# Two layers of a hybrid diffusion backbone: banks, table loads and eviction order in the LRU stage

## The chip, the cores and the metric

One core of a Trainium2 chip runs the whole program in one launch. The metric is the device time of one execution in microseconds (us); several executions are timed and the median is taken. TensorE (PE) multiplies matrices into PSUM banks, VectorE (DVE) and ScalarE (ACT) read them and do the elementwise work, GpSimd (POOL) does little here, and SyncE (SP) issues the transfers. PEld is TensorE's loading of weights.

## What is computed

For 256 latent tokens and 256 context tokens of width 1024, each of two layers does this (the reference, cut; the attention branches and the feed-forward part are left as calls):

```python
h = _rmsnorm(x, lp['norm1_g']) * (1.0 + sc1) + sh1            # hc for the context tokens in the same way
rx, rg, cq, ckv, kr, dq, dk, dv, mg = _split_cols(h @ lp['w_in'], IN_SPLITS)
# RG-LRU branch
xr = _centred_dwconv(rx, lp['conv_w'], lp['conv_b'])
r = jax.nn.sigmoid(gr);  i = jax.nn.sigmoid(gi)               # gr, gi: block-diagonal products of xr
log_a = -LRU_C * r * jax.nn.softplus(-lam)
a = jnp.exp(log_a)
b = jnp.sqrt(-jnp.expm1(2.0 * log_a)) * i * xr
y_a = scan_forward(a[0], b[0]) + scan_backward(a[1], b[1])
# merge of the three branches
br_a = (y_a * jax.nn.gelu(rg)) @ lp['w_br_a']
br_b = o_b @ lp['w_br_b']                                      # latent attention
br_c = oc @ lp['w_br_c']                                       # differential attention
ga, gb, gc = jnp.split(jax.nn.sigmoid(mg), N_BRANCH, axis=-1)
x = x + g1 * ((ga * br_a + gb * br_b + gc * br_c) @ lp['w_out'])
x = x + g2 * _ffn(...)
```

The last layer needs the context tokens only as keys, values and start of the recurrence, so most of its products have 256 columns where the first layer's have 512.

## The kernel before

All products are made in split precision: `wload` fetches a weight block of 128x1024 float32, ACT copies it to a rounded half (`wh`) and DVE subtracts to get the rest (`wl`, both at L131 in `split`), and `mm3` (L192 to L194) issues three matmuls for each tile. A ring of three blocks (`WB`) holds weights; in the last layer two more lie in `room`, with two more staging blocks in the space of `acc`. A new block's transfer waits in SP's queue until DVE has split the block that used the same staging tile. Weight copies and splits are put 90 places ahead of program order (`WEIGHTS_FIRST`). The order of each engine's queue is made at build time by a scheduler that takes the ready instruction with the lowest order number; `tc.cur_priority` shifts that number. Once made, each engine runs its queue in order.

`gemm_fm` computes 256 output channels (two tiles j) over two weight blocks. In layer 0 (512 columns) the two tiles take a PSUM bank each, in layer 1 (256 columns) both share one, except rx's, which always has 512 columns. PSUM has eight banks: three with tag "mm" (`ps_mm`), two with tag "tr" (`ps_tr`, used by transposes), and three of a stage's own (`three_banks`).

The stage that the change is about comes after the differential attention's stage (the "pair" stage) and is called "single" (L1141). It loops over four pairs p of tiles. `rnn_rx` computes the recurrence's input for pair p+1 and `rnn_conv` evicts and convolves it (L1017 copies the bank to `xr` in layer 0, L1022 reads it). `rnn_rg` first runs `rnn_rec`: the two gates' products into the stage's own banks `pg`, Tanh (L1041), Exp (L1045), Tanh (L1046), then for the four results of the pair a Sqrt each (L1058), then multiplications (L1062) and scans (L1068) on DVE. Then it computes rg's product, and `gelu2` evicts it: Square (L1006, ACT), a product with the bank (L1007, DVE), Tanh (L1008, ACT), a product with the bank again (L1009, DVE). Between these, a queue of generators is worked off (`fill`): `branch_proj`, the differential branch's projection, read from its bank by DVE at L1107 together with its gate, and `branch_gate`, whose bank ACT reads with a Tanh into `gt` at L1099. The first gate and the first rx are already queued in the pair stage. All of these blocks use `ps_mm`. In layer 0 a slow background task (`mod_vectors`, L302) shares DVE.

ACT's functions come in table sets. The square root is in another set than Tanh and Exp, and a load is put by the compiler before the first function that needs another set. Copies, squares and the like need no particular set.

Of the kernel before, what the change touches and what calls it, by code (L numbers as in the profile page):

```python
# [13 lines left out]
AF = mybir.ActivationFunctionType  # L14
# [9 lines left out]
T = SEQ + CTX  # L24
# [32 lines left out]
WEIGHTS_FIRST = 90  # L57
NORMS_FIRST = 300
PAIR_FIRST = 2000


@with_exitstack
def tile_hybrid(ctx: ExitStack, tc: tile.TileContext, xt, cvec, cwide, prm, row, dlam, rope, wmod, wmod0, wmodt, wfm, wcq, wckv, wuq, wukv, wlru, wfo, out):
# [46 lines left out]
        return banks[0].tile([P, 512], F32, tag="sc", name=name, bufs=singles[0])  # L110

    turn = [0]

    def ps_any(name):

# [104 lines left out]
    def issue_after(b, a):  # L220

        tc.add_manual_dep(b.ins, a.ins.name, mybir.DependencyInfo(mybir.DependencyClass.NoSync, mybir.DependencyReason.DATA), reason="one table for all")
# [161 lines left out]
    def gemm_fm(l, widx, npair, xH, xL, TQ, ps_, consume, k_first=False):  # L384

        one = 2 * TQ <= 512
        for p in range(npair):
            if one:
                ps = ps_("ps0").rearrange("p (j n) -> p j n", j=2)
                pss = [ps[:, j, :] for j in range(2)]  # L390
            else:
                pss = [ps_(f"ps{j}")[:, :TQ] for j in range(2)]
            for hf in range(2):
                H, L = wload(*fm_block(l, widx, 2 * p + hf))
                H = H.rearrange("p (k n) -> p k n", n=256)
                L = L.rearrange("p (k n) -> p k n", n=256)
                order = [(j, kk) for kk in range(4) for j in range(2)] if k_first and p == 0 else [(j, kk) for j in range(2) for kk in range(4)]
                for i, (j, kk) in enumerate(order):
                    k = hf * 4 + kk
                    mm3(pss[j], H[:, kk, j * P:(j + 1) * P], L[:, kk, j * P:(j + 1) * P], xH[:, k, :TQ], xL[:, k, :TQ],  # L400
                        k == 0 and not (one and j == 1), k == KT - 1 and not (one and j == 0), one)
                    if k == KT - 1:
                        if not one:
                            consume(2 * p + j, 1, pss[j].unsqueeze(1))
                        elif j == 1:
                            consume(2 * p, 2, ps)
                    if i % 4 == 3 or k_first and p == 0 and i % 2 == 1:
                        yield (6 if k_first and p == 0 else 12) * mm_ns(TQ)
# [126 lines left out]
    for l in range(LAYERS):  # L535
# [7 lines left out]
        with ExitStack() as c1:  # L543
# [13 lines left out]
            def t_cq(name, dt=F32R):  # L557
                return tmp("cq", 10, dt=dt, name=name)
# [4 lines left out]
            def t_p(name):  # L563
                return tmp("p", 4, name=name)
# [448 lines left out]
            def rnn_conv(t, ps, st):  # L1013
                xr = ps
                if not last:
                    xr = t_p("xr")
                    A.activation(xr, ps, AF.Copy)  # L1017
                xc = t_cq("xc", F32)
                xr3 = xr.rearrange("p (s t) -> p s t", s=2)
                xc3 = xc.rearrange("p (s t) -> p s t", s=2)  # L1020
                w = [pm[:, CW + 8 * j + t:CW + 8 * j + t + 1] for j in range(4)]
                A.activation(xc, xr, AF.Identity, scale=w[2], bias=pm[:, CB + t:CB + t + 1])  # L1022
                for j in (0, 1, 3):
                    o_ = j - 2
                    d0, d1 = max(0, -o_), SEQ - max(0, o_)
                    V.scalar_tensor_tensor(out=xc3[:, :, d0:d1], in0=xr3[:, :, d0 + o_:d1 + o_], scalar=w[j], in1=xc3[:, :, d0:d1], op0=ALU.mult, op1=ALU.add)
                xH, xL = t_qk("xH"), t_qk("xL")
                split(xH, xL, xc)
                st.append((t, xc, xH, xL))

            def rnn_rec(pair, H, L):

                four = []
                for t, xc, xH, xL in pair:
                    for r in range(2):
                        th = []
                        for z in range(2):
                            pg = ps_sc("pg")
                            mm3(pg, H[:, z, r, t % 2, :], L[:, z, r, t % 2, :], xH, xL, True, True)
                            tz = t_pt("tz", F32)  # L1040
                            A.activation(tz, pg, AF.Tanh, scale=0.5, bias=hb[:, z, r, t:t + 1])  # L1041
                            th.append(tz)
                        a, tn = t_cq("a", F32), th[0]
                        sp = nsp[:, r, t:t + 1]
                        A.activation(a, th[0], AF.Exp, scale=sp, bias=sp)  # L1045
                        A.activation(tn, th[0], AF.Tanh, scale=sp, bias=sp)  # L1046
                        a2 = t_sc()
                        if last:
                            V.tensor_tensor(out=a2, in0=a, in1=a, op=ALU.mult)
                        else:  # L1050
                            A.activation(a2, a, AF.Square)
                        root = V.scalar_tensor_tensor(out=tn, in0=a2, scalar=1.0, in1=tn, op0=ALU.add, op1=ALU.mult)
                        g = xc if r else t_cq("g", F32)
                        V.scalar_tensor_tensor(out=g, in0=th[1], scalar=1.0, in1=xc, op0=ALU.add, op1=ALU.mult)
                        four.append((t, r, a, tn, g))
                        yield 6 * mm_ns(T)
                for t, r, a, tn, g in four:
                    issue_after(A.activation(tn, tn, AF.Sqrt, scale=-0.25), root)  # L1058
                lat, cx = slice(0, SEQ), slice(SEQ, T)
                hs = {}  # L1060
                for t, r, a, tn, g in four:
                    V.tensor_tensor(out=tn, in0=tn, in1=g, op=ALU.mult)  # L1062
                    hh = t_v("hh", F32)
                    for sl, h0 in ((cx, 0.0), (lat, hh[:, T - 1:T] if r == 0 else hh[:, SEQ:SEQ + 1])):
                        o_, a_, b_ = hh[:, sl], a[:, sl], tn[:, sl]
                        if r == 1:
                            o_, a_, b_ = o_[:, ::-1], a_[:, ::-1], b_[:, ::-1]
                        V.tensor_tensor_scan(out=o_, data0=a_, data1=b_, initial=h0, op0=ALU.mult, op1=ALU.add)  # L1068
                    if r == 0:
                        hs = hh  # L1070
                    else:
                        V.tensor_tensor(out=hs[:, :TQ], in0=hs[:, :TQ], in1=hh[:, :TQ], op=ALU.add)
                        st_y[t] = hs

            st_y = {}

            def rnn_rx(p, st):
                yield from gemm_fm(l, W_RX + p, 1, hH, hL, T, ps_mm, lambda j, n, ps: rnn_conv(2 * p + j, ps[:, 0, :], st))

            def rnn_rg(p):  # L1080
                H, L = wload(wlru[l, p])
                H = H.rearrange("p (z r n d) -> p z r n d", z=2, r=2, n=2)
                L = L.rearrange("p (z r n d) -> p z r n d", z=2, r=2, n=2)
                ge = {}
                yield from rnn_rec(rst[p], H, L)
                yield from gemm_fm(l, W_RG + p, 1, hH, hL, TQ, ps_mm, lambda j, n, ps: gelu2(j, n, ps, ge))
                for j in range(2):
                    t = 2 * p + j
                    V.tensor_tensor(out=ge[j], in0=ge[j], in1=st_y[t][:, :TQ], op=ALU.mult)
                    nc.sync.dma_start(yspill[:, t, :TQ], ge[j])  # L1090
# [4 lines left out]
            def branch_gate(mgi, p):  # L1095
                def gate(j, n, ps):
                    gt = t_v("gt", F32)[:, :n * TQ].rearrange("p (n c) -> p n c", n=n)
                    gts[mgi, 2 * p + j] = gt
                    A.activation(gt, ps, AF.Tanh, scale=0.5)  # L1099

                yield from gemm_fm(l, W_MG + mgi * 4 + p, 1, hH, hL, TQ, ps_mm, gate)

            def branch_proj(widx, mgi, p, after=None):
                def proj(j, n, ps):
                    t = 2 * p + j
                    gt = gts.pop((mgi, t))
                    V.scalar_tensor_tensor(out=gt, in0=gt, scalar=1.0, in1=ps, op0=ALU.add, op1=ALU.mult)  # L1107
                    V.tensor_tensor(out=acc[:, t:t + n, :TQ], in0=acc[:, t:t + n, :TQ], in1=gt, op=ALU.add)
                    if after is not None:
                        after(t + n - 1)  # L1110

                yield from gemm_fm(l, widx + p, 1, oH, oL, TQ, ps_mm, proj)

            three_banks(f"pair{l}")
            singles[0] = 1
# [24 lines left out]
            flush()  # L1140
            three_banks(f"single{l}")  # L1141
            singles[0] = 3

            c2.close()
            if not last:
# [322 lines left out]
```

## Time and profile before

| | |
|---|---|
| median of 3 runs | 1986.53 us (1986.1 to 1989.13) |
| the profiled execution | 1987.02 us |
| its span, first to last instruction | 1985.2 us |
| PE busy | 1935.7 us, 98% |
| DVE busy | 1570.4 us, 79% |
| ACT busy | 1070.8 us, 54% |
| POOL busy | 58.9 us, 3% |

All times in rows are from the start of the span. Matmuls are pipelined and their modelled ends overlap, so a PE that is busy all the time need not be at its peak. In a timeline, a row is a run of like instructions of one engine, and the bracket gives the idle time of the engine before it and whose signal ended that. A wait for several signals is put down to the one that came last. Layer 0's pair stage ends at about 555 us and its single stage runs from there; layer 1's single stage begins at about 1600 us.

### The profile page before, as it was taken

Reading aid. Unit: us, or ns where it says so; the run is one execution under the profiler, and the core shown is the slowest. Engines: PE = TensorE matmul, PEld = TensorE weight load, DVE = VectorE, ACT = ScalarE, POOL = GpSimd, SP = SyncE. Lnnn points to the kernel's source line nnn. Section 1 sums busy time; section 2 is a strip of 40 time slices with the busy share of each in tenths; the row PEclk is TensorE's granted clock in tenths of the full one; section 3 lists DMA queues with packets and bytes.
Section 4 is the critical chain, followed back from the end, with each engine's and each line's share of the span. In section 5 each row is a group of like instructions: output and inputs, shape, how many; then the busy total and the mean of one; then the engine's idle time right before and its main releaser. Section 6 shows DMA issues by size and latency. Waiting matters only on the chain. (4 is left out here: it accounts for less than half of the span.)

```text
span 1985.2 us, 31873 instructions
## 1 busy us (share of the span) xinstructions
PE 1935.7 (98%) x11746; PEld 1667.6 (84%) x11746; DVE 1570.4 (79%) x3870; ACT 1070.8 (54%) x1975; POOL 58.9 (3%) x198
## 2 busy tenths in 40 slices
PE   7999999999999999999999999999999999899999
PEld 4888888988677778888888888988999788898888
DVE  5679965888797787879888766898688889966763
ACT  4578833555576672343223224798444578855552
POOL 0001000000000000000000000012010000000000
PEclk9999999999999999999999999999999999999999
DMA  7211122112133356536665653412422134464553
GB/s 293 95 41 50 54 64 86 65 55 86 49 114 126 116 182 196 195 109 204 195 200 192 202 180 115 155 59 84 127 89 83 61 116 144 153 229 159 181 191 107
DMA packets 92028, 258.16 MB, mean 130 GB/s; under 512 B 10336, under 2 KB 17504, under 8 KB 91872
## 3 DMA queue, kind: packets, MB, share of 16 engines
q1 hardware_dynamic: 91872, 256.13, 39.2%
q8 instruction: 92, 1.51, 0.3%
q14 instruction: 64, 0.52, 0.1%
HBM read 250.85 MB, written 5.24 MB: 129 GB/s over the span
## 5 line engine op out<-in xcount | busy, mean ns | idle before, releaser
L131 ACT ACTIVATE wh<-st 128x1024 fp32r<-128x1024 f32 (+4 forms) x305 | 308.4, 1013 | 387.4 <-PE ps L193 188.6
L131 DVE TENSOR_TENSOR wl<-st,wh 128x1024 fp32r<-128x1024 f32 (+4 forms) x305 | 353.9, 1162 | 138.1 <-ACT wh L131 135.0
L192 PE MATMUL ps<-hH,wh 128*128 128x512 f32 (+1 forms) x512 | 187.3, 366 | 11.5 <-ACT gt L1099 8.8
L194 PE MATMUL ps<-hH,wl 128*128 128x512 f32 (+1 forms) x512 | 185.5, 363 | 4.5 <-DVE wl L131 4.5
L193 PE MATMUL ps<-hL,wh 128*128 128x512 f32 (+1 forms) x512 | 186.0, 363 | 0.0
L192 PE MATMUL pst<-wh,hH 128*128 128x256 f32 x568 | 164.4, 289 | 0.0
L193 PE MATMUL pst<-wl,hH 128*128 128x256 f32 x568 | 162.1, 285 | 0.0
L194 PE MATMUL pst<-wh,hL 128*128 128x256 f32 x568 | 162.0, 285 | 0.0
L192 PE MATMUL ps<-h2H,wh 128*128 128x512 f32 (+1 forms) x368 | 139.1, 381 | 0.6 <-ACT h2H L371 0.6
L193 PE MATMUL ps<-h2L,wh 128*128 128x512 f32 (+1 forms) x368 | 139.5, 380 | 0.0
L194 PE MATMUL ps<-h2H,wl 128*128 128x512 f32 (+1 forms) x368 | 139.5, 380 | 0.0
L613 DVE TENSOR_REDUCE st<-S 128x1 f32<-128x512 f32 (+1 forms) x192 | 112.9, 596 | 23.2 <-ACT dp L615 11.6
L192 PEld LDWEIGHTS ps<-hH,wh 128*128 128x128 f32 x512 | 98.4, 192 | 29.4 <-ACT gt L1099 10.9
L194 PEld LDWEIGHTS ps<-hH,wl 128*128 128x128 f32 x512 | 98.4, 192 | 19.7 <-DVE wl L131 5.9
L192 PEld LDWEIGHTS pst<-wh,hH 128*128 128x128 f32 x568 | 108.6, 191 | 3.8 <-issue 3.3
L131 DVE TENSOR_TENSOR room<-acc,room 128x1024 fp32r<-128x1024 f32 (+3 forms) x75 | 87.4, 1168 | 29.6 <-ACT room L131 28.3
L194 PEld LDWEIGHTS pst<-wh,hL 128*128 128x128 f32 x568 | 108.5, 191 | 1.7 <-issue 1.4
L193 PEld LDWEIGHTS ps<-hL,wh 128*128 128x128 f32 x512 | 98.6, 193 | 13.1
L193 PEld LDWEIGHTS pst<-wl,hH 128*128 128x128 f32 x568 | 108.6, 191 | 1.1 <-issue 0.7
L302 DVE SCALAR_TENSOR_TENSOR ms<-ms,cb 128x512 f32<-128x512 f32 x160 | 107.1, 686 | 1.3
L131 ACT ACTIVATE room<-acc 128x1024 fp32r<-128x1024 f32 (+3 forms) x75 | 76.2, 1017 | 57.0 <-PE ps L193 20.9
L302 DVE SCALAR_TENSOR_TENSOR sq<-ms,cb 128x512 f32<-128x512 f32 x112 | 75.5, 688 | 31.1 <-DMA ms<-wmodt 30.4
(586 smaller groups left out, 5542.6 us busy)
## 6 DMA issues: line engine op xcount, KB each, us to landing
st<-wfm SPq DMA_DIRECT2D x224, 512.0 KB, 3.5
ms<-wmodt SPq DMA_DIRECT2D x160, 256.0 KB, 2.8
acc<-wfm SPq DMA_DIRECT2D x56, 512.0 KB, 3.5
st<-wfo SPq DMA_DIRECT2D x35, 512.0 KB, 3.5
mstage<-wmod SPq DMA_DIRECT2D x16, 512.0 KB, 5.4
acc<-wfo SPq DMA_DIRECT2D x9, 512.0 KB, 3.5
st<-wlru SPq DMA_DIRECT2D x7, 512.0 KB, 3.4
st<-wukv SPq DMA_DIRECT2D x13, 256.0 KB, 2.5
```

The lines of the kernel that those rows point to most:

```text
L131: return A.activation(dH, src, AF.Copy), V.tensor_tensor(out=dL, in0=src, in1=f(dH), op=ALU.subtract)
L192: nc.tensor.matmul(ps, wH, xH, start=start, stop=False, skip_group_check=skip)
L193: nc.tensor.matmul(ps, wH, xL, start=False, stop=False, skip_group_check=skip)
L194: nc.tensor.matmul(ps, wL, xH, start=False, stop=stop, skip_group_check=skip)
L302: issue_after(V.scalar_tensor_tensor(out=o, in0=st, scalar=1.0, in1=cb[:, v, :], op0=ALU.mult, op1=ALU.mult, accum_out=sums[:, i - i0, h, ...
L613: V.tensor_reduce(out=st[:, 0:1], in_=S, axis=AX.X, op=ALU.max, negate=True)
```

## The change

Three things are changed, all for the blocks of the single stage.

The load of the table set with Tanh and Exp is written out, ordered behind the last of a group's four square roots, in `rnn_rec`.

rx, rg, gate and projection blocks take their banks in turn from five (`ps_five`: mm, tr, mm, tr, mm) from the start of the single stage on. Blocks started before, in the pair stage, keep `ps_mm`.

The order numbers of three kinds of evictions are lowered by 400 (`EVICT_FIRST`): the copy of rx's bank in layer 0, the gates' Tanh and the projections' read at L1107. The sum into `acc` behind that stays where it was.

```diff
+EVICT_FIRST = 400
...
+    five = [0]
+
+    def ps_five(name):
+
+        five[0] += 1
+        return (ps_mm, ps_tr, ps_mm, ps_tr, ps_mm)[(five[0] - 1) % 5](name)
...
                 if not last:
                     xr = t_p("xr")
+                    tc.cur_priority -= EVICT_FIRST
                     A.activation(xr, ps, AF.Copy)
+                    tc.cur_priority += EVICT_FIRST
...
                 for t, r, a, tn, g in four:
-                    issue_after(A.activation(tn, tn, AF.Sqrt, scale=-0.25), root)
+                    sq_ = A.activation(tn, tn, AF.Sqrt, scale=-0.25)
+                    issue_after(sq_, root)
+                issue_after(nc.scalar.preload_act_table_set("exp_and_others"), sq_)
...
+            ps_r = [ps_mm]
 
             def rnn_rx(p, st):
-                yield from gemm_fm(l, W_RX + p, 1, hH, hL, T, ps_mm, lambda j, n, ps: rnn_conv(2 * p + j, ps[:, 0, :], st))
+                yield from gemm_fm(l, W_RX + p, 1, hH, hL, T, ps_r[0], lambda j, n, ps: rnn_conv(2 * p + j, ps[:, 0, :], st))
...
-                yield from gemm_fm(l, W_RG + p, 1, hH, hL, TQ, ps_mm, lambda j, n, ps: gelu2(j, n, ps, ge))
+                yield from gemm_fm(l, W_RG + p, 1, hH, hL, TQ, ps_r[0], lambda j, n, ps: gelu2(j, n, ps, ge))
...
+                    tc.cur_priority -= EVICT_FIRST
                     A.activation(gt, ps, AF.Tanh, scale=0.5)
-
-                yield from gemm_fm(l, W_MG + mgi * 4 + p, 1, hH, hL, TQ, ps_mm, gate)
+                    tc.cur_priority += EVICT_FIRST
+
+                yield from gemm_fm(l, W_MG + mgi * 4 + p, 1, hH, hL, TQ, ps_r[0], gate)
...
+                    tc.cur_priority -= EVICT_FIRST
                     V.scalar_tensor_tensor(out=gt, in0=gt, scalar=1.0, in1=ps, op0=ALU.add, op1=ALU.mult)
+                    tc.cur_priority += EVICT_FIRST
...
-                yield from gemm_fm(l, widx + p, 1, oH, oL, TQ, ps_mm, proj)
+                yield from gemm_fm(l, widx + p, 1, oH, oL, TQ, ps_r[0], proj)
...
             three_banks(f"single{l}")
             singles[0] = 3
+            ps_r[0] = ps_five
```

## Rows read from the trace of the kernel before

**Rows 1.** The page's first part: busy us, share of the span, instructions.

```profile
PE 1935.7 (98%) x11746; PEld 1667.6 (84%) x11746; DVE 1570.4 (79%) x3870; ACT 1070.8 (54%) x1975; POOL 58.9 (3%) x198
```

**Rows 2.** Busy time by stretch: stretch, us, then each engine (instructions), clock, DMA.

```profile
core 0: us, PE busy (x) PEld busy (x) DVE busy (x) ACT busy (x) POOL busy (x), PEclk, DMA share, GB/s
555.00:790.00 235.00, 225.07 (x967) 181.76 (x966) 198.41 (x361) 142.62 (x208) 0.00 (x0) 0.99 0.45 148
1600.00:1725.00 125.00, 115.20 (x764) 104.46 (x764) 119.21 (x175) 105.50 (x146) 0.00 (x0) 1.00 0.40 131
```

**Rows 3.** PE's waits, 500 to 800 us: total us, times, longest.

```profile
PE ps L192 <- ACT gt L1099: 8.8, 5, 2.8
PE ps L192 <- DVE gt L1107: 2.7, 1, 2.7
```

**Rows 4.** Timeline of PE at the four longest of these: start, us, what.

```profile
529.57 0.50 PE L192 MATMUL ps<-hH,wh 128*128 128x512 f32 x1 [2.17 <-ACT gt L1099]
...
586.00 0.50 PE L192 MATMUL ps<-hH,wh 128*128 128x512 f32 x1 [2.83 <-ACT gt L1099]
...
638.78 0.50 PE L192 MATMUL ps<-hH,wh 128*128 128x512 f32 x1 [2.83 <-ACT gt L1099]
...
728.02 0.66 PE L192 MATMUL ps<-hH,wh 128*128 128x512 f32 x1 [2.67 <-DVE gt L1107]
```

**Rows 5.** PE's waits in layer 1's stage, 1590 to 1740 us.

```profile
PE ps L194 <- DVE room L131: 4.7, 3, 1.7
PE ps L194 <- DVE wl L131: 4.5, 2, 3.0
```

**Rows 6.** Busy time by stretch, 3.3 us behind PE's long waits (clock after POOL).

```profile
530.20:533.50 3.30, 3.30 (x13) 2.26 (x11) 1.26 (x4) 2.17 (x4) 0.00 (x0) 0.50 0.59 197
586.00:589.30 3.30, 3.30 (x14) 2.73 (x15) 2.80 (x4) 0.90 (x2) 0.00 (x0) 1.00 0.48 129
639.40:642.70 3.30, 3.30 (x9) 2.55 (x8) 3.30 (x8) 0.34 (x1) 0.00 (x0) 0.50 0.46 164
728.20:731.50 3.30, 3.30 (x9) 2.53 (x9) 3.30 (x6) 0.63 (x1) 0.00 (x0) 0.50 0.36 137
...
1724.90:1728.20 3.30, 3.30 (x18) 3.30 (x17) 3.30 (x7) 2.19 (x4) 0.00 (x0) 0.50 0.56 166
```

**Rows 7.** Timeline of DVE around 586 us: weight splits, ge's last reader.

```profile
586.40 1.20 DVE L131 TENSOR_TENSOR wl<-st,wh 128x1024 fp32r<-128x1024 f32 x1
...
589.50 0.69 DVE L1009 SCALAR_TENSOR_TENSOR ge<-ge,ps 128x512 f32<-128x512 f32 x1 [0.70 <-ACT ge L1008]
...
590.83 1.22 DVE L131 TENSOR_TENSOR wl<-st,wh 128x1024 fp32r<-128x1024 f32 x1
```

**Rows 8.** Timeline of ACT around 528 us and around 583 us.

```profile
527.21 1.06 ACT L131 ACTIVATE wh<-st 128x1024 fp32r<-128x1024 f32 x1 [2.19 <-PE ps L193]
528.18 0.76 ACT L615 ACTIVATE dp<-S,st,drq 128x512 f32<-128x512 f32 x1
...
528.93 0.58 ACT L1099 ACTIVATE gt<-ps 128x512 f32<-128x512 f32 x1
...
576.80 1.66 ACT L1058 ACTIVATE tz<-tz 128x512 f32<-128x512 f32 x3
581.17 0.60 ACT L1006 ACTIVATE ge<-ps 128x512 f32<-128x512 f32 x1 [2.71 <-PE ps L194]
582.98 1.06 ACT L131 ACTIVATE wh<-st 128x1024 fp32r<-128x1024 f32 x1 [1.22 <-PE ps L193]
584.05 1.28 ACT L1099 ACT_TABLE_LOAD   x1
585.35 1.09 ACT L1099 ACTIVATE gt<-ps 128x512 f32<-128x512 f32 x2
```

**Rows 9.** By line, whole span: busy us, mean ns; L1107: min/median/max ns.

```profile
L1058 ACT ACT_TABLE_LOAD x8 | 10.3, 1283 | 0.1
L1099 ACT ACT_TABLE_LOAD x4 | 5.1, 1283 | 0.1
...
L1107 DVE SCALAR_TENSOR_TENSOR gt<-gt,ps x24: 657/682/687, 568.2 to 1763.5; 128x512 f32<-128x512 f32 x24
```

## The prediction

> **What bounds the kernel now.** I read the busy shares first, then PE's waits, then the timelines around the longest waits, then the granted clock behind them. PE is busy for 98% of the span [rows 1], so only its gaps and its slow stretches can be won back. The change touches two stages. In layer 0's LRU stage (555 to 790 us) PE is busy 225.07 of 235 us, DVE 198.41 and ACT 142.62; in layer 1's (1600 to 1725) PE 115.20 of 125, DVE 119.21 and ACT 105.50 [rows 2]. So layer 0 is a PE stage with some idle gaps, and layer 1 is a DVE stage (95% busy) in which PE waits for DVE.
>
> The waits say the same. Around layer 0's stage PE waited 8.8 us in five pieces for ACT's read of a gate (gt, L1099) and 2.7 us once for DVE's read of a branch projection (gt, L1107) [rows 3]. The waiting matmul reads hH and wh and writes a fresh ps, and neither operand is made by L1099 or L1107: it waits for a PSUM bank. The four long pieces end at 529.57, 586.00, 638.78 and 728.02 us and last 2.17, 2.83, 2.83 and 2.67 us [rows 4]; the other gate pieces are 8.8 - 7.83 = 0.97 us together. In layer 1 PE waited for no bank: 4.7 and 4.5 us went to weight splits on DVE (room, wl) [rows 5].
>
> A long wait costs more than its length. Behind 529.57, 638.78 and 728.02 the granted clock is 0.50 (1.2 instead of 2.4 GHz) for at least 3.3 us, and behind layer 1's 3.0 us wait too; behind 586.00 it is 1.00 [rows 6]. In 3.3 us at half clock PE does 1.65 us of work, so each such stretch costs 1.65 us. (The matmul counts, 9 against 14, agree roughly; records can be missing.)
>
> **Why the banks come late.** Three "mm" banks serve blocks that take two banks each in layer 0. ge's chain (L1006 to L1009) holds a bank longest: its last reader begins at 589.50 [rows 7], although its first read is at 581.17 [rows 8]. That leaves too few for a gate block beside it. The gate's eviction itself is late: ACT runs a weight copy at 582.98, a table load of 1.28 us at 584.05 and only then the two gates at 585.35, and PE restarts at 586.00 [rows 4, 8].
>
> **The change part by part.**
>
> *Five banks in the single stage.* No instruction is added; rx, rg, gate and projection blocks rotate over 3 mm + 2 tr banks. The tr banks belong to transposes of the stages before, so no reader of this stage loses one. With ge holding two, three are left for blocks that need two and that are evicted within some 3 us, while a block lasts 5.5 us (14.5 matmuls in 3.3 us [rows 6] is 0.228 us each, x24). The next block's second bank is due 12 matmuls, 2.7 us, after its first. I take the three waits in the single stage as gone: 2.83 + 2.83 + 2.67 = 8.33 us, and the two half-clock stretches behind them, 3.30 us: **-11.6 us**. From below: none goes, if something else is due at the same moment (first rival). From above: 11.6, as a wait cannot go below nothing.
>
> What is late next is the weights. PE without the wait begins at 583.2 the block that it now begins at 586.00, and needs the next split at 588.7. DVE begins it at 586.40 and takes 1.20, so it is there at 587.6; the one after is begun at 590.83, done at 592.05, and needed at 594.2 [rows 7]. The lead is only 1.1 and 2.1 us, and DVE is 84% busy, so I give back 0.5 us for each of the four passes, **+2.0 us** (bounds 0, and 8.33, one wait for another).
>
> *The table load behind the square roots.* Each of 8 groups of square roots costs one load there and one back at the first Tanh (1.283 us each [rows 9]). The explicit load takes the place of the second, so the number stays 16, and ACT's busy time too. It moves: at 578.46 ACT has finished its roots and idles 2.71 us until PE releases ge [rows 8], so layer 0's load is covered. In layer 1 ACT is 84% busy and weight copies follow the roots; there the load holds up the copies and splits behind it by up to 1.28 us, four times. DVE, the fuller engine, has other work queued then; I cost it at nothing, up to 4 x 1.28 = 5.1 us if that cover is gone, and down to -1.28 x 3 where a gate no longer has the load in front of it. The gain for gates in layer 0 is already in the waits above.
>
> In the trace the gate's load begins as the copy ends and the gate begins as the load ends: 582.98 + 1.06, then 584.05 + 1.28, then 585.35 [rows 8], so a switch costs 1.28 us here. The Trainium skill ("ScalarE: Activation LUTs", What ACT_TABLE_LOAD costs) states about 1283 ns plus a drain of about 1380 ns, some 2.66 us in all; by that each of the 4 loads now at L1099 would be worth about 1.4 us more, and the sum would be some 1970 us. The trace shows no such drain, and the sum goes by 1.28.
>
> *Evictions ahead of weight blocks.* EVICT_FIRST lowers the order number of the xr copies (ACT, 8, layer 0 only), gate Tanhs (ACT, 24) and projection reads (DVE, 24 of 0.68 us [rows 9]) by 400, beyond the 90 of the weights. Nothing is added; an eviction that is ready together with a weight copy or a softmax Exp goes first. It also reaches the pair stage, which keeps three banks: at 528.93 the gate stands behind a weight copy (527.21) and an Exp with its accumulator read (528.18, which holds ACT for 0.75) [rows 8]. The copy was ready first and I leave it ahead. That wins 0.75 of the 2.17 us, and the remaining 1.4 us is shorter than any wait behind which [rows 6] show half clock, so 1.65 more; the 0.97 us of small pieces I halve: 0.75 + 1.65 + 0.49 = **-2.9 us** (from 0 to 2.17 + 1.65 + 0.97 = 4.8). What is passed is the cost. In layer 1 each eviction that goes ahead of a split for which PE waits adds 0.6 to 0.7 us. There are five such waits [rows 5]; I take two as hit, 2 x 0.68 = **+1.4 us** (bounds: five hit, 3.4, each with a half-clock stretch, 8.3 more; or two fewer waits, -1.4). The DMA queue issues a weight load when DVE's split frees a stage, so a split 0.68 us later puts its load 0.68 us later; that is in the same figure.
>
> **Sum.** -11.6 + 2.0 - 2.9 + 1.4 = -11.1 us. The profiled execution took 1987.02 us (span 1985.2), 0.5 us above the median of 1986.53. So 1975.9 for an execution like it, **1975.4 us** for the median.
>
> **Rivals.**
>
> *Weight waits take the place of bank waits (0.14).* For it: leads of 1.1 and 2.1 us, and DVE's scans stand in front of splits. Against it: ACT's copy at 582.98 waited for PE to free a weight buffer, so weights are ahead when the wait begins. If PE gets 8.33 us back from banks and waits as long for splits, with the clock falling as now, only -2.9 + 1.4 stays: 1985 us, within 0.2%. The Trainium skill ("TensorE: Matmul & The Clock Gate", HAM oscillation) tells of a kernel where "Adding PSUM double-buffering gave no further gain". By that rule the time would be this rival's; layer 1, where PE waits for splits alone, agrees with it, layer 0's rows don't.
>
> *Layer 1's weights get later (0.14; slower).* Place: ACT and DVE from 1600 to 1725. Up to 8 gates of 0.6 and 8 projections of 0.68 us pass weight work there, 10.2 us, and four loads of 1.28 stand ahead of copies. DVE is 95% busy, so a split that is passed isn't caught up. Price: 10.2 + three half-clock stretches, 5.0, + 5.1 = 20 us. It decides from where that exceeds layer 0's 12.5 us, that is if over 60% of these land before a due split; slower by over 0.2% takes 16 of the 20; all of them: 1994 us. Against it: the total of DVE's work is unchanged, and only five splits were late.
>
> *A gate's Tanh goes between the square roots (0.06).* With 400 in hand a gate can be chosen ahead of a root; each time costs two extra loads, 2.57 us of ACT ahead of the scans. In layer 1 four of these cost 10.3 us: about 1986 us, no measurable change. Against it: in the pass shown the gates come 6.9 us after the last root [rows 8].
>
> *The evictions don't move (part of the forecast).* If each is queued where it was, the five banks alone leave 1978 us or so.
>
> **How the numbers follow.** The forecast has 0.66, with its own range 1968 (all bank waits and stretches gone, nothing given back) to 1982. The other three hold 0.34; of them 0.02 falls short of its price and stays faster. For 8 in 10 the range reaches over the weight-wait rival: 1968 to 1987. A measurement of this kernel can tell about 0.2%, 4 us. Faster than 1982.6: 0.68; within 0.2%: 0.18; slower than 1990.5: 0.14.
>
> **What would show it.** Right: PE's waits for L1099 and L1107 gone in 555 to 790 us, no stretch at half clock there, PE over 98% of that stage; 8 loads on the new line and none at L1099, L1008 or L1041; layer 1's waits for room and wl within 2 us of 9.2. Wrong: waits for wl or room in layer 0 of more than 4 us, more than 16 loads around the roots, or DVE idle falling to nothing in layer 1 with PE's waits above 12 us.

## The result, and the profile after

| | before | after |
|---|---|---|
| median | 1987.83 us (1986.1 to 1991.39) | 1997.93 us (1996.68 to 2000.06) |
| after / before | | 1.0051 [1.0038, 1.0064] |
| the profiled execution, span | 1987.02 us, 1985.2 us | 1998.22 us, 1996.4 us |

The forecast was 1975.4 us and faster. The kernel became 10.1 us slower. So two things have to be found: whether the 11 us that were promised came at all, and where some 22 us went.

The first part of the page (busy us, share of the span, instructions) shows the same numbers of instructions as [rows 1], and PE's share is one point lower:

```profile
PE 1939.1 (97%) x11746; PEld 1672.9 (84%) x11746; DVE 1572.2 (79%) x3870; ACT 1071.9 (54%) x1975; POOL 58.9 (3%) x198
```

PE's busy time is 3.4 us longer than in [rows 1] for the same work (the mean granted clock of the execution is 0.991, before 0.995), the span 11.2 us. So most of the loss is idle time of PE. Stage by stage, beginning with the one that the prediction spoke of: busy time by stretch in the kernel after (columns as in [rows 2]):

```profile
541.00:561.00 20.00, 9.67 (x41) 7.73 (x42) 13.16 (x43) 8.26 (x28) 0.00 (x0) 0.69 0.00 1
575.00:800.00 225.00, 221.95 (x973) 181.83 (x972) 192.28 (x341) 140.18 (x198) 0.00 (x0) 1.00 0.50 154
820.00:873.00 53.00, 49.16 (x252) 41.60 (x251) 33.26 (x68) 18.09 (x25) 0.00 (x0) 0.97 0.43 140
```

The same view of the kernel before, at the stretches that answer to the first and the third line:

```profile
541.00:561.00 20.00, 19.80 (x100) 15.20 (x99) 18.03 (x49) 15.24 (x40) 0.00 (x0) 1.00 0.27 86
816.00:864.00 48.00, 48.00 (x258) 41.26 (x257) 29.37 (x58) 18.82 (x27) 0.00 (x0) 1.00 0.40 138
```

The second line of after is the single stage of layer 0, and there the forecast came true: PE is busy 221.95 of 225 us at clock 1.00 (before, 215.07 us of the same stretch at 0.98). The first line is the end of the pair stage, just ahead of it: PE falls from 19.80 busy us to 9.67, the clock from 1.00 to 0.69, and the DMA traffic from 86 to 1 GB/s, so not even a weight block is fetched. The third is the output projection of layer 0, just behind the stage: 3.84 us idle, clock 0.97, where PE never stopped before.

PE's waits in the kernel after, 500 to 830 us (total us, times, longest):

```profile
PE subt L1006 <- DVE so L999: 5.7, 1, 5.7
PE ptr L637 <- DVE dp L965: 3.2, 1, 3.2
PE subt L991 <- ACT so L988: 2.3, 2, 1.6
PE ps L199 <- ACT gt L1112: 2.1, 2, 1.4
PE ps L201 <- DVE wl L138: 1.5, 1, 1.5
PE ps L199 <- ACT wh L138: 1.1, 1, 1.1
PE po L984 <- ACT pH L138: 0.7, 1, 0.7
PE pg L199 <- ACT tz L1050: 0.5, 1, 0.5
```

Against [rows 3]: the 8.8 us for gates (L1099, now L1112) are 2.1, both before 541 us, and the 2.7 us for a projection (L1107, now L1122) are gone. In their place stand 5.7, 3.2, 2.3 and 0.7 us for the pair stage's own chain: DVE's scaled tiles `so`, ACT's halves `pH`, the transposes `subt` and `ptr`. That chain is no slower than before (from the `subt` transposes at 541.81 us to the last at 564.99 it took 23.2 us, now 541.02 to 559.85, 18.8); what is new is that PE has nothing else to do while it waits. The timeline of PE (start us, us, what) shows what it ran there, and what came behind:

```profile
541.02 0.66 PE L991 MATMUL subt<-ident,so 128*128 128x128 f32 x4 [1.61 <-ACT so L988]
...
545.16 0.44 PE L637 MATMUL ptr<-ident,dp 128*128 128x128 f32 x1 [3.16 <-DVE dp L965]
...
559.85 1.11 PE L1006 MATMUL subt<-ident,so 128*128 128x128 f32 x4 [5.73 <-DVE so L999]
560.61 0.78 PE L199 MATMUL ps<-hH,wh 128*128 128x512 f32 x1
```

And PE's groups from 541 to 561 us in the kernel before (busy us, mean ns | idle before), five of its sixteen groups:

```profile
L193 PE MATMUL ps<-hL,wh 128*128 128x512 f32 x9 | 3.7, 410 | 0.0
L192 PE MATMUL ps<-oH,wh 128*128 128x512 f32 x9 | 3.7, 408 | 0.0
L194 PE MATMUL ps<-hH,wl 128*128 128x512 f32 x9 | 3.6, 401 | 0.0
L193 PE MATMUL ps<-oL,wh 128*128 128x512 f32 x9 | 3.5, 394 | 0.0
...
L192 PE MATMUL pg<-xH,wh 128*128 128x512 f32 x4 | 1.7, 416 | 0.0
```

Before, blocks that belong to the single stage (rx and gate read hH, projections oH, the recurrence's gates xH) filled the gaps of the pair stage's tail: the scheduler had drawn them forward over the stage's border. After, the only block instruction in that stretch is the one at 560.61 us, right behind the last transpose of the pair stage. The kernel's text suggests why: the first block that takes its banks from the five is rx of the second pair, its second bank is a "tr" bank, and the bank's earlier tiles in program order are the transposes of the pair stage's end, the last being `subt` at L1006. Then the scheduler, which places instructions at build time, would place that block behind those, and the blocks after it too. The rows show the order; the reason is a theory that the runs have to test.

### The profile page after: what moved, and what is told of

Same layout as the page of the kernel before. It is cut to its first block, busy times and chain, and to the rows that moved or that the text cites. A ratio compares the mean times of both kernels' runs of the same rounds, so it can differ in the third digit from the quotient of the medians.

```text
span 1996.4 us, 31857 instructions
## 1 busy us (share of the span) xinstructions
PE 1939.1 (97%) x11746; PEld 1672.9 (84%) x11746; DVE 1572.2 (79%) x3870; ACT 1071.9 (54%) x1975; POOL 58.9 (3%) x198
## 5 line engine op out<-in xcount | busy, mean ns | idle before, releaser
L620 DVE TENSOR_REDUCE st<-S 128x1 f32<-128x512 f32 (+1 forms) x192 | 113.1, 597 | 21.9 <-ACT dp L622 11.6
L309 DVE SCALAR_TENSOR_TENSOR ms<-ms,cb 128x512 f32<-128x512 f32 x160 | 107.3, 688 | 1.2
L309 DVE SCALAR_TENSOR_TENSOR sq<-ms,cb 128x512 f32<-128x512 f32 x112 | 76.0, 690 | 37.4 <-DMA ms<-wmodt 36.8
```

The source lines that it names most:

```text
L309: issue_after(V.scalar_tensor_tensor(out=o, in0=st, scalar=1.0, in1=cb[:, v, :], op0=ALU.mult, op1=ALU.mult, accum_out=sums[:, i - i0, h, ...
L620: V.tensor_reduce(out=st[:, 0:1], in_=S, axis=AX.X, op=ALU.max, negate=True)
```

## The experiments

The first theory (**banks at the border**): the whole loss comes of the "tr" banks, because the first single-stage blocks wait for the last transposes. Its rivals: the evictions that pass weight work, or the moved table loads, cost it in layer 1, as the prediction had feared. The first four runs take one edit each, and all three with the banks later.

**e1_table**: only the explicit table load.

```diff
-                    issue_after(A.activation(tn, tn, AF.Sqrt, scale=-0.25), root)
+                    sq_ = A.activation(tn, tn, AF.Sqrt, scale=-0.25)
+                    issue_after(sq_, root)
+                issue_after(nc.scalar.preload_act_table_set("exp_and_others"), sq_)
```

> Only the table load is moved behind the square roots. Bank theory (the first blocks of the single stage wait for the two tr banks of the pair stage's last transposes): nothing of the loss is here, 1984 to 1990 us, and PE's gate waits at 586 and 639 us shorten by up to 1.3 us each. Eviction theory (the loss comes from evictions that pass weight work): the same. Table theory (the load holds up weight copies): 1992 us or more.

Measured: 1985.97 us, 0.9995 [0.9986, 1.0005], no change. PE's timeline at two of the gate waits, 2.83 us each in [rows 4]:

```profile
584.87 0.50 PE L192 MATMUL ps<-hH,wh 128*128 128x512 f32 x1 [1.41 <-ACT gt L1101]
...
637.23 0.50 PE L192 MATMUL ps<-hH,wh 128*128 128x512 f32 x1 [1.41 <-ACT gt L1101]
```

Each is 1.42 us shorter, about the 1.28 us of the load that no longer stands in front of the gate. PE's first matmul of layer 0's output projection (`ps<-mH`) comes 4.90 us sooner than before. Then it is given back: 1.46 us in that projection and 3.2 us in layer 1's single stage, where a wait of 2.1 us for the recurrence's Tanh on ACT and a stretch at clock 0.57 (1699.5 to 1707 us) appear; PE's first matmul of layer 1's output projection is back to 0.14 us ahead of before. So the edit works where the prediction said, and is worth nothing over the whole.

**e2_five**: only the five banks (the lines of `ps_five` and `ps_r` in the change).

```diff
+            ps_r[0] = ps_five
```

> Only the five banks. Bank theory: the whole loss is here, 1995 to 2001 us, with PE standing in layer 0 between 541 and 561 us for 11 to 13 us and at half clock for some 17 us there, and the gate and projection waits of 586 to 728 us gone. Eviction theory: those waits gone and no stop at 541 to 561 us, 1972 to 1980 us.

Measured: 1989.4 us, 1.001 [1.0001, 1.0019]. PE's waits, 530 to 565 us, in this kernel:

```profile
PE subt L1006 <- DVE so L999: 5.7, 1, 5.7
PE ptr L637 <- DVE dp L965: 3.2, 1, 3.2
PE subt L991 <- ACT so L988: 1.4, 2, 0.7
PE po L984 <- ACT pH L138: 0.7, 1, 0.7
```

The stop at the border is there with this edit alone (PE is busy 9.73 us from 541 to 561, in the changed kernel 9.67), and the gate waits of the single stage are gone. But the time is 5.6 us under the 1995 that the first theory wanted at least, so it is not the whole loss.

**e3_evict**: only the evictions ahead of weights.

```diff
+                    tc.cur_priority -= EVICT_FIRST
                     A.activation(gt, ps, AF.Tanh, scale=0.5)
+                    tc.cur_priority += EVICT_FIRST
```

(and so for the xr copy and the projection's read)

> Only the evictions ahead of weight blocks, with the three old banks. Bank theory: 1982 to 1988 us, the 2.2 us gate wait at 529.6 us shorter by 0.75 and no half clock behind it, no stop at 541 to 561 us. Eviction theory: 1993 us or more, with PE's stop at 541 to 561 us.

Measured: 1984.55 us, 0.9984 [0.9974, 0.9993], a small gain. The wait of 2.17 us at 529.57 in [rows 4], and the 3.3 us behind it (0.50 in [rows 6]), in this kernel:

```profile
529.09 0.50 PE L199 MATMUL ps<-hH,wh 128*128 128x512 f32 x1 [1.41 <-ACT gt L1110]
```

```profile
529.20:532.50 3.30, 3.30 (x18) 2.47 (x18) 2.24 (x6) 2.32 (x6) 0.00 (x0) 1.00 0.80 221
```

2.17 - 1.41 = 0.76 us won and no half clock, as the prediction had worked out (0.75 and 1.65). There is no stop at 541 to 561 us here.

**e4_late**: all three edits, the five banks from the second pass of the single stage on.

```diff
-            ps_r[0] = ps_five
...
             for p in range(4):
+                if p == 1:
+                    ps_r[0] = ps_five
                 queue.append(branch_proj(W_BC, 2, p))
```

> All three edits, but the blocks that are started in the first of the four passes keep the three mm banks; the five begin with the second pass. Bank theory: the stop at 541 to 561 us is gone (12 us of waits and some 8 us of clock), the waits of the later passes stay gone: 1975 to 1983 us. Eviction or table theory: 1993 us or more.

Measured: 1983.27 us, 0.9975 [0.9966, 0.9985], 14.7 us under the changed kernel and 0.3 us above the range that the first theory gave. Stretches of this kernel, the border and the output projection:

```profile
541.00:561.00 20.00, 19.82 (x100) 15.33 (x99) 17.64 (x46) 15.25 (x40) 0.00 (x0) 1.00 0.25 70
...
806.00:857.00 51.00, 48.95 (x250) 41.33 (x249) 32.62 (x66) 18.03 (x25) 0.00 (x0) 0.97 0.45 145
```

The stop is gone with the tr banks out of the first pass: 19.82 busy us, clock 1.00. That settles the border. But the second stretch has lost 2.05 us of idle time and some half clock. Two more places of PE's timeline, this kernel first and then the changed kernel:

```profile
809.76 0.50 PE L199 MATMUL ps<-mH,wh 128*128 128x512 f32 x1 [2.05 <-DVE gt L1122]
```

```profile
838.50 0.52 PE L199 MATMUL ps<-mH,wh 128*128 128x512 f32 x1 [3.84 <-DVE x L1207]
```

In both, a matmul of the output projection, which still takes its banks from the three "mm", waits for a bank that DVE has to read. In e4 that is the read of a branch projection (L1122), which DVE begins at 809.01 us, without a pause before it, behind reads of the background task (L309) and a weight split; DVE's pause of 3.09 us for the background task's transfer comes later there (to 821.71 us) and costs PE nothing. In the changed kernel it is such a pause (timeline of DVE):

```profile
831.37 1.22 DVE L138 TENSOR_TENSOR wl<-st,wh 128x1024 fp32r<-128x1024 f32 x1
...
835.93 0.69 DVE L309 SCALAR_TENSOR_TENSOR junk<-ms,cb 128x512 f32<-128x512 f32 x1 [3.34 <-DMA ms<-wmodt]
...
837.49 1.65 DVE L1207 SCALAR_TENSOR_TENSOR x<-ps,mod,x 128x256 f32<-128x256 f32 x4
```

DVE idles 3.34 us in front of an instruction of the background task (`mod_vectors`, L309 here), which waits for its transfer, and the four residual reads (L1207) that would free PE's banks stand behind it in the queue. The Trainium skill ("PSUM — Partial Sum Buffer", Engine vs sequencer instructions) calls the queues of ScalarE, VectorE and GpSimd strict FIFO; this row agrees, with 3.84 us of PE's time. A second theory follows: **output banks**. As PE comes to the projection earlier relative to DVE's background task, three banks no longer bridge DVE's delay. The first theory's rest can also be an edit's own fault, so the next runs ask both.

**e5_tabfive** and **e8_fiveevict**: the changed kernel without the evictions, and without the explicit table load.

```diff
-                    tc.cur_priority -= EVICT_FIRST
...
-                    tc.cur_priority += EVICT_FIRST
```

(e5; three times)

> Table load and five banks from the first pass on, evictions in their old order. The five banks alone took 1989.4 us and all three edits 1997.9, with the same stop at 541 to 561 us in both. If the evictions passing weight work make the other 8 us: 1988 to 1992 us here. If the early table load makes them: 1995 to 2000 us.

```diff
-                issue_after(nc.scalar.preload_act_table_set("exp_and_others"), sq_)
```

(e8)

> Five banks from the first pass on and the evictions, without the early table load. If the evictions make the other 8 us: 1995 to 2000 us. If the table load makes them: 1986 to 1991 us. If it takes both, through the place that the output projection then has against DVE's background work: under 1992 us here and in the run without evictions alike.

Measured: e5 1993.88 us, 1.0029 [1.0019, 1.004]; e8 1991.55, 1.002 [1.001, 1.003]. With e2's 1989.4 and 1997.93 for all three, each edit that is good or harmless alone adds 2 to 6 us on top of the five banks. So neither of the two is at fault by itself (e5 lies in neither of the ranges expected of it), and this pair doesn't tell why they add up. The wait in the output projection is in all of them, and shorter than the 3.84 us of the changed kernel: 2.13 us in e2, 2.60 in e5, 2.49 in e8. The traces do tell where the 9.2 us between the spans of e2 and of the changed kernel arise: 3.6 us ahead of layer 0's output projection, 3.3 us in it and 2.3 us behind it. In the projection it is the wait and the clock behind it. The clock doesn't fall behind e2's wait, and is 0.50 for at least 3.3 us behind those of e8 and of the changed kernel and 6.6 us behind e5's; the projection takes 2.4 us longer than before in e2, 4.1 in e8, 5.7 in the changed kernel and 5.8 in e5.

**e6_out5**: e4, and layer 0's output projection takes its banks from the five.

```diff
-                for i, _ in enumerate(gemm_fm(l, W_OUT, 3, mH, mL, TQ, ps_mm, out_tile, True)):
+                for i, _ in enumerate(gemm_fm(l, W_OUT, 3, mH, mL, TQ, ps_five, out_tile, True)):
...
-                gemm_halves(l, W_OUT + 3, mH, mL, ps_mm, half_tile, False, half_norm)
+                gemm_halves(l, W_OUT + 3, mH, mL, ps_five, half_tile, False, half_norm)
```

> The kernel with five banks from the second pass on, with the output projection of layer 0 on the five banks as well. If the 2.2 us wait at 810 us and the half clock behind it (3.9 us together) come from too few banks while DVE is late with evictions: they are gone and the time is 1978 to 1981 us. If DVE is late with the projection's data and not only with its banks: the wait stays, 1982 to 1985 us.

Measured: 1978.68 us, 0.9955 [0.994, 0.997]. The projection, and the border, in this kernel:

```profile
541.00:561.00 20.00, 19.80 (x100) 15.42 (x99) 17.65 (x47) 15.73 (x39) 0.00 (x0) 1.00 0.31 91
...
805.00:852.00 47.00, 47.00 (x251) 40.30 (x250) 33.09 (x68) 17.84 (x25) 0.00 (x0) 1.00 0.49 159
```

PE no longer stops in the projection: 47.00 of 47 us at clock 1.00. The edit is worth 1983.27 - 1978.68 = 4.6 us. DVE waits as long as before for the background task's transfer (3.48 us, in e4 3.09); with two banks more PE doesn't notice. The execution in e6's trace is the fastest of its four (1976.53 us), so what is read from it is some 2 us better than its median.

**e7_best** and **e9_best2**: e6 with the explicit load in layer 0 alone (as e1 had lost in layer 1), and e7 with layer 1's part of the change varied further: five banks from the first pass there, no eviction ahead.

```diff
+                if not last:
                     issue_after(nc.scalar.preload_act_table_set("exp_and_others"), sq_)
```

(e7)

> As the run beside it, with the early table load in layer 0 alone. The early load alone lengthened layer 1's stage by 3.2 us; if the load ahead of weight copies does that, 1975 to 1979 us here, 2 to 3 us under the run beside it; if the load is harmless there, no difference.

```diff
-                if p == 1:
+                if p == (0 if last else 1):
...
-                    tc.cur_priority -= EVICT_FIRST
+                    tc.cur_priority -= 0 if last else EVICT_FIRST
```

(e9)

> Five banks from the second pass on in layer 0 and from the first in layer 1, evictions first and early table load in layer 0 alone, output projection of layer 0 on five banks. The version with evictions first in layer 1 took 1976.5 us and its stage in layer 1 was as long as before; the five banks alone shortened that by 1.5 us. If the evictions take that back: 1974 to 1976 us. If not: 1976 to 1978 us.

Measured: e7 1976.52 us, 0.9944 [0.9929, 0.9959]; e9 1976.35, 0.9946 [0.9931, 0.9961]. Both beat the kernel before and the changed one. From e6 to e7 it is 2.2 us, and their intervals overlap; between e7 and e9 there is no difference, so in layer 1 the early start of the five banks together with unmoved evictions costs nothing that can be told. The loss at the border is layer 0's; why layer 1 has none isn't shown.

**e10_early_out5** and **e11_mmfirst**: the changed kernel with five banks for the output projection (e6's edit alone), and the same with the "mm" banks handed out first.

```diff
-        return (ps_mm, ps_tr, ps_mm, ps_tr, ps_mm)[(five[0] - 1) % 5](name)
+        return (ps_mm, ps_mm, ps_mm, ps_tr, ps_tr)[(five[0] - 1) % 5](name)
```

(e11, besides e10's edit)

> The changed kernel (five banks from the first pass on) with the output projection of layer 0 on five banks too. The kernel with five banks from the second pass on took 1978.7 us with that edit and 1983.3 without. Bank theory: the stop at 541 to 561 us stays, the one at 838 us (5.7 us with its clock) is gone: 1991 to 1994 us, 13 to 15 us over the later start. If the two stops are one and the same lateness: 1982 us or less.

> As the run beside it, with the five banks in the order mm, mm, mm, tr, tr, so that the first rx block has no tr bank and the next projection has one. Bank theory, whichever block asks for the first tr bank stops behind the last transposes: rx's 48 matmuls fill part of the time, the stop is shorter but not gone, 1980 to 1989 us. If only the number of banks counts: as the run beside it.

Measured: e10 1993.43 us, 1.0028 [1.0018, 1.0038]; e11 1983.0, 0.998 [0.997, 0.9989]. The border in e10, and then in e11:

```profile
541.00:561.00 20.00, 9.74 (x39) 7.75 (x39) 12.89 (x41) 8.64 (x27) 0.00 (x0) 0.71 0.00 1
```

```profile
541.00:561.00 20.00, 18.06 (x86) 12.70 (x84) 17.16 (x46) 15.21 (x40) 0.00 (x0) 1.00 0.21 66
```

e10 and e6 differ only in when the five banks begin. That costs 1993.43 - 1978.68 = 14.75 us; by the traces 13.1 us of it are there when PE begins layer 0's output projection. The edit of the output projection is worth 1997.93 - 1993.43 = 4.5 us, as between e4 and e6. In the trace the projection alone is 5.7 us shorter in e10 than in the changed kernel; ahead of it e10 is 2.2 us earlier, with less half clock at the border (mean clock 0.80 from 541 to 575 us, in the changed kernel 0.75), and behind it 1.8 us are lost again. e11 takes the same five banks as early as e10, and only the order in which they are handed out differs: the first rx block then gets "mm" banks, the stop shrinks from 10.3 idle us to 1.9, and 10.4 of the 14.75 us come back. Part of the stop has moved behind 561 us: from 541 to 575 us PE idles 3.9 us in e11, 10.3 in e10 and 1.8 in e6. The stop is thus made by which bank the first blocks get, not by the number of banks or by the early start as such.

## Why the prediction failed, point by point

PE's first and last matmul of layer 0's output projection, and the end of the span, against the kernel before (816.80, 863.04 and 1985.22 us), from the timelines:

| kernel | first | last | end |
|---|---|---|---|
| after | +4.1 us | +9.8 us | +11.2 us |
| e4 (five banks from the second pass) | -9.9 us | -5.9 us | -3.3 us |
| e10 (after, five banks for the projection) | +1.9 us | +1.9 us | +5.0 us |
| e6 (both) | -11.2 us | -11.2 us | -10.5 us |

**The step that failed** is the sentence "The tr banks belong to transposes of the stages before, so no reader of this stage loses one". As to readers it holds. But it looked at the banks from the stage's inside, and forgot that the stage's first blocks run during the stage before: [rows 4] have a gate block's matmul at 529.57, in the pair stage, and in the kernel before the scheduler drew others into the stage's tail. Those that ran between 541 and 561 us came to need a bank that the pair stage's transposes held to their end. By the rows this is 10.1 us of PE's idle time more (19.80 - 9.67), and, from 545.3 to 552.0 and from 555.6 to 565.6 us, 11.7 busy us at clock 0.50, of which half, 5.9, is lost:

```profile
545.30:552.00 6.70, 5.97 (x21) 4.70 (x22) 3.52 (x10) 2.87 (x5) 0.00 (x0) 0.50 0.00 0
555.60:565.60 10.00, 5.75 (x16) 4.69 (x17) 4.53 (x17) 1.32 (x2) 0.00 (x0) 0.50 0.01 2
```

Together that is 16 us. The kernels with the later start idle a little behind the border instead: by 575 us PE was busy 32.23 of 34 us in e4 and 23.67 in the changed kernel, so 8.6 us of idle time and the 5.9 us are to be expected between these two, 14.4 us, and PE's first matmul of the output projection is 14.0 us later (13.1 between e10 and e6). The prediction had no rival for this: the only one that it called slower lay in layer 1. None of the signs of being wrong that it named appeared.

**What it didn't foresee besides** is the output projection behind the stage, 4.5 us (after against e10). It had asked what is late next for weights alone; the next three-bank stage, whose evictions share DVE's queue with a background task, wasn't asked. The timelines of all kernels agree on what counts there. Take as PE's lead the time from its first matmul of the projection to the background read for whose transfer DVE pauses in the projection:

| kernel | first matmul | background read | lead | PE's wait for the residual read |
|---|---|---|---|---|
| before | 816.80 | 827.19 | 10.4 us | none |
| e1 | 811.90 | 824.30 | 12.4 us | 1.22 us |
| e3 | 812.26 | 825.11 | 12.9 us | 1.24 us |
| e2 | 817.32 | 830.63 | 13.3 us | 2.13 us |
| e8 | 816.72 | 830.39 | 13.7 us | 2.49 us |
| e5 | 817.42 | 831.20 | 13.8 us | 2.60 us |
| after | 820.90 | 835.93 | 15.0 us | 3.84 us |
| e10 (five banks there) | 818.71 | 833.86 | 15.2 us | none |
| e6 (five banks there) | 805.58 | 821.14 | 15.6 us | none |

With three banks the wait grows with the lead, with five there is none. (e4's lead of 14.9 us holds an earlier wait of 2.05 us and half clock behind it; DVE's pause cost PE nothing there.) Why the lead differs from kernel to kernel isn't shown.

**Five banks inside the stage: right.** From 575 to 800 us PE's waits went from 9.9 us (5.9 and 2.7 for gates and a projection, 0.9 and 0.4 others) to 3.1 (1.5, 1.1 and 0.5 in the waits of after). So 8.6 us of bank waits left, forecast 8.33, and 3.1 - 1.3 = 1.8 us of others came, forecast 2.0; as this is mainly one wait of 1.5 us for a split and not 0.5 us in each of four passes, the match is in part luck. The granted clock is 1.00 over the whole stretch, so both half-clock stretches went too. The rival that weights would take the place of the banks is refuted in this stage: DVE was 85% busy there (192.28 of 225 us) and the splits were at most 1.5 us late. The Trainium skill ("Perfetto Trace Analysis", Matmuls) advises that independent groups rotate over different PSUM banks, so that one's evacuation overlaps the next one's matmuls. By the 575 to 800 us row, with 8.6 us of bank waits gone, the trace agrees; the 541 to 561 us row shows the price where a bank in the rotation is still owned by an earlier stage.

**Table loads: moved as said, and worth nothing over the whole.** By line (busy us, mean ns | idle before) the kernel after has 8 loads at the roots and 8 at the new line, and none at the Tanhs of the gates, of `gelu2` or of the recurrence:

```profile
L1067 ACT ACT_TABLE_LOAD x8 | 10.3, 1283 | 0.1
L1069 ACT ACT_TABLE_LOAD x8 | 10.3, 1283 | 0.1
```

e1's gate waits became 1.42 us shorter each, about one load, so the drain that the Trainium skill ("ScalarE: Activation LUTs", What ACT_TABLE_LOAD costs) adds to it isn't seen in them either. In layer 1 the load costs something, as its upper bound (5.1 us) allowed: e1 lost 3.2 us in layer 1's single stage.

**Evictions: right in layer 0** (0.76 us against 0.75, no half clock behind it), and e3's whole gain, 2.3 us, fits the -2.9 + 1.4 by sign and about by size. In e3's trace PE begins the output projection 4.5 us earlier than before and loses 1.9 us in it, and layer 1 adds 0.2 us. **Layer 1: the sum right within its bounds.** PE's waits there in the kernel after, 1590 to 1760 us:

```profile
PE ps L201 <- DVE wl L138: 3.3, 2, 2.3
PE ps L201 <- DVE room L138: 2.5, 2, 1.6
PE pg L199 <- ACT tz L1050: 2.0, 3, 1.0
PE ps L199 <- ACT o L140: 1.4, 1, 1.4
PE ps L199 <- ACT room L138: 0.6, 1, 0.6
```

PE waits 3.4 us less for splits than the 9.2 of [rows 5], more than the 2 us that the prediction gave as a sign of being right, and waits for ACT (tz, o, room) have come up in their place; the sum is 9.8 us. From the end of layer 0's projection to layer 1's last W_OUT matmul the shift grows by 0.8 us, where +1.4 was forecast. The rival that layer 1's weights get later (up to 20 us) didn't happen; that the result is slower as it had said is no support for it.

**The sum.** Where the two unforeseen costs are removed (e6), PE begins the output projection 11.2 us earlier than before, where the steps for layer 0 had summed to -11.6 + 2.0 - 2.9 = -12.5. With the loads left out of layer 1 (e7) the time is 1976.5 us, 1.1 us from the forecast. That closeness is partly luck, as e7 is not the kernel that was forecast; the 9.9 to 11.2 us by which PE begins layer 0's output projection earlier in e4, e6 and e7 are the fairer measure. So the gain in layer 0 was sized about right and the cost was missed. Split by edits, the 1997.93 - 1976.52 = 21.4 us between the changed kernel and e7 are 14.75 (start of the five banks), 4.5 (banks of the output projection) and 2.2 (load in layer 1, not clear of noise). One figure beside the sum doesn't follow from its terms: if the evictions don't move, their +1.4 doesn't come either, and -11.6 + 2.0 gives 1976.9 us, not 1978. What stays open is why each edit on top of the early start costs more than alone (e2, e5, e8, after), and the 4.3 us between e11 and e6, which by the traces are there (4.5 us) when PE begins the output projection.

## What to carry to other kernels

Banks borrowed from an earlier stage aren't free from the borrower's first instruction on: where a build-time scheduler draws the next stage's blocks into the tail of the one before, those blocks must not take a bank whose last owner sits at the very end of that tail. Hand out the borrowed banks last, or a pass later, and look at the trace on both sides of the border, not only at the stage that the banks are for. And when a stage gets faster, ask which evictions of the next one stand in an in-order queue behind work or a transfer that doesn't get faster with it.

## What the runs showed of the hardware that was not expected

The prediction charged 1.65 us for each stretch at half clock, from 3.3 us stretches [rows 6]. Behind several waits in a row the clock stayed at 0.50 for longer: 6.7 and 10.0 us in the two rows above, the second beginning during the wait of 5.7 us. A matmul of 128x512 then followed the one before at 0.43 us instead of 0.23 (561.18, 561.61, 562.04 us in after's timeline, 555.68, 555.91, 556.15 in before's). In the changed kernel a stretch in layer 1 lasted as long, though PE idled only 2.1 us in it:

```profile
1729.70:1736.40 6.70, 4.61 (x21) 4.62 (x22) 6.70 (x10) 3.36 (x6) 0.00 (x0) 0.50 0.46 138
```

A row of waits isn't needed for it either: in e5's output projection PE had one wait, of 2.60 us, and the clock was 0.50 from 833.20 to 839.80 us, while it stayed at 1.00 behind e2's 2.13 us, and behind the 2.83 us of [rows 6] at 586 us. So a price per stretch read from one kernel's rows need not hold in another.
